# Splitting q and k for the attention scores: three float32r products on row halves in place of one float32 product

## The chip, the cores and the metric

The kernel runs on one core of a Trainium2 chip. The metric is device time in microseconds (us) of one execution; lower is better. TensorE (PE) does the matrix products, VectorE (DVE), ScalarE (ACT) and GpSimd (POOL) the elementwise work, SyncE (SP) issues the DMAs. PEld is the loading of a product's stationary operand.

## The reference

One decoder layer over 16 meta tokens and 1024 tokens, width 1024. A normalized input is projected; half of the result feeds a state-space scan (SSD), the other half stick-breaking attention with 16 heads of 64. Both are normalized and projected out, then comes a gated feed-forward part with a short convolution. The change lies in the attention scores, `zlog` below:

```python
def block(args):                       # one block of 128 queries
    i, qi = args
    zlog = jnp.einsum('bqhd,bkhd->bhqk', qi, kp) * scale
    log_beta = jax.nn.log_sigmoid(zlog)
    log_keep = jnp.where(valid, log_beta - zlog, 0.0)
    after = lax.cumsum(log_keep, axis=3, reverse=True) - log_keep
    w = jnp.where(valid, jnp.exp(log_beta + after), 0.0)
    return jnp.einsum('bhqk,bkhd->bqhd', w, vp)
```

All inputs and the output are float32.

## The kernel before

The large projections are already done in split form: an operand is rounded to float32r (the high part), the rest is a second float32r tile, and three products (high x high, rest x high, high x rest) are summed in PSUM in place of one float32 product (`project_steps`, line 163). The attention scores are plain float32 products.

Heads are worked in eight pairs `p`: head 2p lies on partitions 0 to 63, head 2p+1 on 64 to 127 (`halves`). `qkv_steps` projects q, k and v of a pair in three column chunks each; ACT copies each chunk out of its PSUM bank (`psum_mm`, two banks in turn) to `q` and `k` in SBUF (line 256). The projections of later pairs are a generator, `fill`, which the loops advance by half a chunk at a time so that TensorE has work between the steps of other stages. Pair 0 and part of pair 1 are projected during the last scan stage.

The attention stage loops over `p` and over eight blocks `i` of 128 queries. `block_weights(p, i)` computes the scores of both heads against all keys up to the block, in chunks of up to 456 keys: `z` (PSUM, two buffers of two banks, shared with the transposes `tw`) gets one product for each row half (line 612). ACT takes two sigmoids of it (`kp`, line 613; `bt`, line 614), VectorE runs a reversed scan over `kp` (line 617), GpSimd multiplies (`bt`, line 619). Two blocks later `block_turn` transposes the weights on TensorE (`tw`, line 633) and ACT copies them (`th`); `block_mix` multiplies them with v (`av`, line 647). In this stage the order of TensorE's instructions is the order in which they are written; the other engines' order is chosen by the scheduler when the program is built. Each engine runs its list in order.

The attention pool `ap` takes over the SBUF of the scan stage's pool. `hold` (lines 584 to 586), which the scan over `kp` reads, is the first of its tiles that VectorE writes. The scan stage ends with the store `yd<-zk` of its last chunk (line 544).

Of the kernel before, what the change touches and what calls it, by code (L numbers as in the profile page):

```python
# [8 lines left out]
F32 = mybir.dt.float32  # L9
F32R = mybir.dt.float32r  # L10
BF16 = mybir.dt.bfloat16
AF = mybir.ActivationFunctionType
ALU = mybir.AluOpType
# [3 lines left out]
P = 128  # L17
# [3 lines left out]
NM = 16  # L21
L = NM + T
# [4 lines left out]
NT = T // P  # L27
# [16 lines left out]
def key_chunks(n):  # L44
    m = (n + 511) // 512
    w = -(-n // m)
    w += w % 2
    return [(a, min(w, n - a)) for a in range(0, n, w)]
# [3 lines left out]
def tile_layer(ctx: ExitStack, tc: tile.TileContext, x, meta, rows, parts,  # L52
               w_z, w_xbc, w_dt, w_q, w_k, w_v, w_out, w_up, w_down, out):
    nc = tc.nc
    mm = nc.tensor.matmul
# [22 lines left out]
    def psum_zz(name):  # L78
        return stage[0][1].tile([P, 2, 512], F32, tag="zz", name=name, bufs=2)
# [4 lines left out]
    def psum_tp(name):  # L84
        return stage[0][1].tile([P, 4, P], F32, tag="tp", name=name, bufs=tp_bufs[0])
# [100 lines left out]
    def rstd_of(pool, ss, n, rows_, name):  # L186
        ms = pool.tile([P, n], F32, tag="ms", name=f"ms_{name}", bufs=2)
        nc.vector.tensor_scalar(ms[:rows_], ss, 1.0 / D, EPS, op0=ALU.mult, op1=ALU.add)
        r = pool.tile([P, n], F32, tag="rstd", name=f"rs_{name}", bufs=2)
        nc.gpsimd.tensor_tensor(r[:rows_], ms[:rows_], nhalf[:rows_, :n], op=ALU.pow)  # L190
        return r
# [3 lines left out]
    rp = roll.enter_context(tc.tile_pool(name="roll", bufs=2, side="right"))  # L195
# [5 lines left out]
    with tc.tile_pool(name="pre", bufs=3, side="right") as pre:  # L201
        gpre = row_bcast(pre, 0, D, "gpre")
        for i in range(NT + 1):
            nr = NM if i == 0 else P
            c0 = 0 if i == 0 else NM + (i - 1) * P
# [5 lines left out]
            r = rstd_of(pre, ss[:nr], 1, nr, f"pre{i}")  # L211
# [3 lines left out]
            for hf in range(2):  # L215
# [3 lines left out]
                for b in range(4):  # L219
                    k = 4 * hf + b  # L220
                    nc.tensor.transpose(tp[:, b, :nr], xn[:nr, k * P:(k + 1) * P], ident[:nr, :nr])
                dst = (slice(None), slice(4 * hf, 4 * hf + 4), slice(c0, c0 + nr))
# [4 lines left out]
    halves = (slice(0, 64), slice(64, 128))  # L227
    M0 = NM - 2
    meta_q = rp.tile([P, 8, 32], F32, tag="mtq", name="meta_q", bufs=1)
    meta_k = rp.tile([P, 8, NM], F32, tag="mtk", name="meta_k", bufs=1)  # L230
    nc.gpsimd.memset(meta_q, 0.0)
    heads, state = {}, {}
# [11 lines left out]
    def qkv_block(name, evac, halves_):  # L244
        w = weights_of(name)
        for i, _ in enumerate(project_steps(w, P, xh, xl, CH, evac, name, halves_)):
            if halves_ and i == 1:
                weights_of(name, 1)
            yield

    def qkv_steps(p, post):
        q = rp.tile([P, L + 3], F32, tag="rq", name=f"q{p}", bufs=3)
        k = rp.tile([P, L], F32, tag="rk", name=f"k{p}", bufs=3)
        for dst, nm in ((q, "q"), (k, "k")):
            def ev(acc, c0, n, dst=dst):
                nc.scalar.activation(dst[:, c0:c0 + n], acc[:, :n], AF.Copy)

            yield from qkv_block(f"{nm}{p}", ev, p > 1 or (p, nm) == (1, "k"))
        vt = rp.tile([P, L], F32, tag="rt", name=f"vt{p}", bufs=1)

        def evv(acc, c0, n):
            nc.scalar.activation(vt[:, c0:c0 + n], acc[:, :n], AF.Copy)

        v = rp.tile([P, NT + 1, P], F32, tag="rv", name=f"v{p}")
        vc = rp.tile([P, P], F32, tag="vc", name=f"vc{p}")
        heads[p] = q, k, v, vc
        yield from qkv_block(f"v{p}", evv, p > 0)

        def turn_v(part):
            tp = psum_tp(f"vtp{p}_{part}")  # L270
            for b in range(4):
                c0 = (4 * part + b) * P
                nc.tensor.transpose(tp[:, b, :], vt[:, c0:c0 + P], ident)
            nc.scalar.activation(v[:, 4 * part:4 * part + 4, :], tp, AF.Copy)

        def turn_edge():
            edge = rp.tile([P, NT, NM], F32, tag="edge", name=f"edge{p}", bufs=1)
            nc.vector.tensor_copy(edge[:, :NT - 1, :], vt[:, P:NT * P].rearrange("p (t c) -> p t c", c=P)[:, :, :NM])
            nc.vector.tensor_copy(edge[:, NT - 1, :], vt[:, T:L])
            tp = psum_tp(f"vtc{p}")  # L280
            nc.tensor.transpose(tp[:, 0, :], edge.rearrange("p t c -> p (t c)"), ident)
            nc.scalar.activation(vc, tp[:, 0, :], AF.Copy)
            for j in range(2):
                nc.vector.tensor_copy(meta_q[halves[j], p, 4 * p + 2 * j:4 * p + 2 * j + 2], q[halves[j], M0:NM])
            nc.vector.tensor_copy(meta_k[:, p, :], k[:, 0:NM])
            nc.sync.dma_start(out=mvd[:, p, :], in_=v[:NM, 0, :])

        post += [lambda: turn_v(0), lambda: turn_v(1), turn_edge]

    def qkv_flow(p):  # L290
        post = []
        return qkv_steps(p, post), post
# [13 lines left out]
    with tc.tile_pool(name="ssd", bufs=1, side="right") as sp:  # L306
# [96 lines left out]
        for i in range(NT + 1):  # L403
            nr = NM if i == 0 else P
            c0 = 0 if i == 0 else NM + (i - 1) * P
# [15 lines left out]
        q, adt = e, s2  # L421
# [160 lines left out]
    ap = apool.enter_context(tc.tile_pool(name="attn", bufs=1, side="right"))  # L582
# [9 lines left out]
                                pattern=[[-NM * mul, NT], [col, 32]], channel_multiplier=mul)  # L592
    edges, ys_of = {}, {}

    def block_weights(p, i):
        q, k = heads[p][:2]
        nm = f"{p}_{i}"
        if i == 0:
            edges[p] = ap.tile([P, 2, NT, NM], F32, tag="cb", name=f"cb{p}", bufs=2)
            nc.gpsimd.memset(edges[p][:, :, :, NM - 1:], 0.0)  # L600
        t0, n = NM + i * P, NM + (i + 1) * P
        kpt = ap.tile([P, 2, L], F32, tag="kp", name=f"kp{nm}", bufs=2)
        btt = ap.tile([P, 2, L], F32, tag="bt", name=f"bt{nm}", bufs=3)
        kp, bt = kpt[:, :, 0:n], btt[:, :, 0:n]
        chunks = key_chunks(n)
        for ci, (a, w) in enumerate(chunks):
            if ci == 2:
                yield
            z = psum_zz(f"z{nm}_{ci}")
            for j in range(2):  # L610
                h = halves[j]
                mm(z[:, j, :w], q[h, t0:t0 + P], k[h, a:a + w], start=True, stop=True)  # L612
            nc.scalar.activation(kp[:, :, a:a + w], z[:, :, :w], AF.Sigmoid, scale=-QSCALE)  # L613
            nc.scalar.activation(bt[:, :, a:a + w], z[:, :, :w], AF.Sigmoid, scale=QSCALE)  # L614
        m = n - NM
        for j in range(2):
            nc.vector.tensor_tensor_scan(kp[:, j][:, ::-1], kp[:, j][:, ::-1], hold[:, L - n:L][:, ::-1], 0.0,  # L617
                                         op0=ALU.mult, op1=ALU.max)
            nc.gpsimd.tensor_tensor(bt[:, j, 0:m], bt[:, j, 0:m], kp[:, j, 1:m + 1], op=ALU.mult)  # L619
        nc.gpsimd.tensor_tensor(edges[p][:, :, i, 0:NM - 1], bt[:, :, m:n - 1], kp[:, :, m + 1:n], op=ALU.mult)  # L620
        turn.append((p, i, bt))
# [188 lines left out]
    for p in range(8):  # L810
        for i in range(NT):
            if p == 0 and i == 0:
                run(fill, 1)
            block = block_weights(p, i)
            next(block, None)
            if p > 0 and i == 3:
# [56 lines left out]
    op = opool.enter_context(tc.tile_pool(name="outp", bufs=2, side="right"))  # L873
# [538 lines left out]
    for i in range(2, NFF):  # L1412
        q = probs[i]
        n = probs[i + 1] if i + 1 < NFF else None
# [119 lines left out]
    for s in range(n2):  # L1534
        n, a, b, p = steps2[s]
# [28 lines left out]
        for _ in range(2 if s > 5 and s % 2 else 1):  # L1564
            if wload and (wload[0][0] is not None or s > 5):
                pool, nm, k = wload.pop(0)
# [9 lines left out]
        if p == NPR - 1:  # L1576
            for t in (3, 0, 1, 2):
                todo.append(lambda n=n, t=t, acc=banks[t]: evac2(n, t, acc))
            if n == 6:
                for t in range(4):  # L1580
                    todo.append(lambda t=t: nc.vector.tensor_tensor(facc[0, 1, t], facc[0, 1, t], facc[1, 0, t],
                                                                    op=ALU.add))
# [74 lines left out]
```

## Time and profile before

| | |
|---|---|
| median of 3 runs | 1810.84 us (1809.62 to 1811.23) |
| the profiled execution | 1810.72 us |
| its span, first to last instruction | 1809.0 us |
| mean granted TensorE clock | 0.988 |
| busy: PE / PEld | 1734.8 us (96%) / 1490.1 us (82%) |
| busy: DVE / ACT / POOL | 1061.0 (59%) / 831.3 (46%) / 863.3 us (48%) |
| score products `z`, line 612 | 87.0 us busy, 448 records |

The profile is of one execution. A float32 product appears as two records. The busy time of PE counts overlapping records once, and a record runs from the start to the modelled end of a pipelined product, so what a product costs is read from the starts of its successors. A wait is put down to what came last.

### The profile page before, as it was taken

The numbers are of one execution on the slowest core, as the hardware profiler recorded it, in microseconds if no ns is written. First come the engines' busy times: TensorE is split into PE (matmuls) and PEld (weight loads), VectorE is DVE, ScalarE is ACT, GpSimd is POOL, SyncE is SP. The second block draws the span as 40 slices with busy tenths as digits, with TensorE's granted clock in tenths as the row PEclk, the third lists the DMA queues.
The fourth block names the chain that finished last, engine by engine and source line by source line (L and its number), as shares of the span: only waits on it lengthen the run. The fifth ranks groups of instructions, "written<-read, shape, count | busy, mean of one in ns | idle before, by whom it ended". The sixth has DMA issues, their size and how long they took to land. (4 is left out here: it accounts for less than half of the span.)

```text
span 1809.0 us, 27308 instructions
## 1 busy us (share of the span) xinstructions
PE 1734.8 (96%) x10942; PEld 1490.1 (82%) x10942; DVE 1061.0 (59%) x1125; ACT 831.3 (46%) x1373; POOL 863.3 (48%) x613
## 2 busy tenths in 40 slices
PE   6999999999999999999889899899999999999997
PEld 5899889888888888887567578888899998888886
DVE  5651864873553454455731246766666666657988
ACT  5423563544565565565652334543333333344444
POOL 3213753585555565554752223277777776600001
PEclk9999999999999999999999899999999999999999
DMA  4124333231011011011212545222333332196344
GB/s 157 47 71 131 99 114 118 65 94 42 24 37 36 26 46 36 24 48 61 70 54 76 200 140 174 73 97 88 105 111 105 93 112 88 60 327 220 97 122 158
DMA packets 90547, 173.96 MB, mean 96 GB/s; under 512 B 10698, under 2 KB 35818, under 8 KB 90420
## 3 DMA queue, kind: packets, MB, share of 16 engines
q1 hardware_dynamic: 90420, 172.21, 29.7%
q8 instruction: 86, 1.41, 0.3%
q14 instruction: 41, 0.34, 0.1%
HBM read 122.39 MB, written 49.79 MB: 95 GB/s over the span
## 5 line engine op out<-in xcount | busy, mean ns | idle before, releaser
L617 DVE TENSOR_TENSOR_SCAN kp<-kp,hold 128x272 f32<-128x272 f32 (+7 forms) x128 | 206.8, 1657 | 194.7 <-ACT kp L613 104.5
L619 POOL TENSOR_TENSOR bt<-bt,kp 128x256 f32<-128x256 f32 (+7 forms) x128 | 215.0, 1697 | 189.2 <-DVE kp L617 132.9
L1022 POOL TENSOR_TENSOR wl<-wr,wh 128x1024 fp32r<-128x1024 f32 x44 | 110.7, 2524 | 40.7 <-ACT wh L1021 40.7
L1470 PE MATMUL dn<-dl,dh 128*128 128x512 f32 x308 | 119.9, 389 | 0.1
L1470 PE MATMUL dn<-dh 128*128 128x512 f32 x308 | 119.9, 389 | 0.0
L1470 PE MATMUL dn<-dh,dl 128*128 128x512 f32 x308 | 119.8, 389 | 0.0
L1516 POOL TENSOR_TENSOR fms<-fms,nhalf 128x1 f32<-128x1 f32 x8 | 8.5, 1060 | 225.7 <-DMA ar<-fda 186.0
L613 ACT ACTIVATE kp<-z 128x288 f32<-128x288 f32 (+6 forms) x112 | 82.8, 739 | 56.8 <-PE z L612 33.1
L1399 ACT ACTIVATE dh<-ar 128x512 fp32r<-128x512 f32 x77 | 48.7, 632 | 111.5 <-PE dn L1470 88.9
L612 PE MATMUL z<-k,q 64*128 64x144 f32 (+6 forms) x448 | 87.0, 488 | 13.3 <-ACT bt L614 6.0
L1021 ACT ACTIVATE wh<-wr 128x1024 fp32r<-128x1024 f32 x44 | 46.6, 1060 | 114.7 <-PE fX L1079 68.3
L1151 DVE SCALAR_TENSOR_TENSOR ga<-gr,pp,ga 128x1024 f32<-128x1024 f32 x44 | 71.3, 1622 | 34.8 <-ACT ga L1144 34.0
L635 ACT ACTIVATE th<-tw 128x1024 f32<-128x1024 f32 (+2 forms) x96 | 74.7, 814 | 34.9 <-PE tw L633 33.0
L614 ACT ACTIVATE bt<-z 128x288 f32<-128x288 f32 (+6 forms) x112 | 83.0, 741 | 0.0
L633 PE MATMUL tw<-ident,bt 128*128 128x128 f32 x576 | 78.8, 282 | 3.8 <-issue 2.8
L647 PE MATMUL av<-th,v 128*64 128x128 f32 x1152 | 78.3, 281 | 0.0
L647 PEld LDWEIGHTS av<-th,v 128*64 128x64 f32 x1152 | 62.8, 138 | 18.8 <-issue 17.9
L1400 DVE TENSOR_TENSOR dl<-ar,dh 128x512 fp32r<-128x512 f32 x77 | 53.3, 692 | 42.0 <-ACT dh L1399 42.0
L633 PEld LDWEIGHTS tw<-ident,bt 128*128 128x128 f32 x576 | 63.2, 143 | 15.6 <-issue 13.1
L612 PEld LDWEIGHTS z<-k,q 64*128 64x128 f32 x448 | 36.9, 187 | 41.8 <-issue 18.5
L1470 PEld LDWEIGHTS dn<-dh 128*128 128x128 f32 x308 | 57.8, 188 | 12.3 <-ACT dh L1399 0.3
L1470 PEld LDWEIGHTS dn<-dl,dh 128*128 128x128 f32 x308 | 57.8, 188 | 12.3 <-DVE dl L1400 0.4
(546 smaller groups left out, 5749.2 us busy)
## 6 DMA issues: line engine op xcount, KB each, us to landing
wr<-in_w_up SPq DMA_DIRECT2D x44, 512.0 KB
fds<-ga SPq DMA_DIRECT2D x44, 256.0 KB
b<-in_w_down SPq DMA_DIRECT2D x44, 256.0 KB
ar<-fds SPq DMA_DIRECT2D x44, 256.0 KB
fda<-ga SPq DMA_DIRECT2D x33, 256.0 KB
ar<-fda SPq DMA_DIRECT2D x33, 256.0 KB
yk<-yd SPq DMA_DIRECT2D x16, 512.0 KB
zd<-zt SPq DMA_DIRECT2D x8, 520.0 KB
```

What stands on the lines that cost most here:

```text
L612: mm(z[:, j, :w], q[h, t0:t0 + P], k[h, a:a + w], start=True, stop=True)
L613: nc.scalar.activation(kp[:, :, a:a + w], z[:, :, :w], AF.Sigmoid, scale=-QSCALE)
L614: nc.scalar.activation(bt[:, :, a:a + w], z[:, :, :w], AF.Sigmoid, scale=QSCALE)
L617: nc.vector.tensor_tensor_scan(kp[:, j][:, ::-1], kp[:, j][:, ::-1], hold[:, L - n:L][:, ::-1], 0.0, op0=ALU.mult, op1=ALU.max)
L619: nc.gpsimd.tensor_tensor(bt[:, j, 0:m], bt[:, j, 0:m], kp[:, j, 1:m + 1], op=ALU.mult)
L633: nc.tensor.transpose(tw[:, j, b, :], bt[:, j, c0:c0 + P], ident)
L635: nc.scalar.activation(th[:, :, :nb, :], tw[:, :, :nb, :], AF.Copy)
L647: mm(av[halves[j], :], v[:, kb, halves[j]], th[:, j, b, :], start=kb == 0, stop=kb == i)
L1022: nc.gpsimd.tensor_tensor(l, raw, h.bitcast(F32), op=ALU.subtract)
L1151: nc.vector.scalar_tensor_tensor(v, self.g[jj][:, :, i:i + 256], fconv_w[:, j, i:i + 1], v, op0=ALU.mult, op1=ALU.add)
L1400: sub(lo[:, k], raw, hi[:, k].bitcast(F32), op=ALU.subtract)
L1470: mm(banks[t], u[:, 0, c], v[:, 1, :], start=(p == 0 and i == 0), stop=(p == NPR - 1 and i == 2))
```

## The change

`qkv_steps` rounds k to float32r when ACT copies it out of PSUM (`kh`), and VectorE subtracts that from the same PSUM bank to get the rest (`kl`). `split_q` does the like for the 128 columns of q that a block needs: VectorE copies them rounded (`qh`) and subtracts (`ql`), both in two buffers from the pool `ap`. `block_weights` asks for the next block's pieces after its own score products and before its scan; the first block makes its own. Each score chunk is now three float32r products for each row half, alternating between the halves. `meta_k` is added up again from the two parts.

```diff
     def qkv_steps(p, post):
         q = rp.tile([P, L + 3], F32, tag="rq", name=f"q{p}", bufs=3)
-        k = rp.tile([P, L], F32, tag="rk", name=f"k{p}", bufs=3)
-        for dst, nm in ((q, "q"), (k, "k")):
+        kh = rp.tile([P, L], F32R, tag="rk", name=f"kh{p}", bufs=3)
+        kl = rp.tile([P, L], F32R, tag="rkl", name=f"kl{p}", bufs=3)
+        for dst, nm in ((q, "q"), (kh, "k")):
             def ev(acc, c0, n, dst=dst):
                 nc.scalar.activation(dst[:, c0:c0 + n], acc[:, :n], AF.Copy)
+                if dst is kh:
+                    nc.vector.tensor_tensor(kl[:, c0:c0 + n], acc[:, :n], kh[:, c0:c0 + n].bitcast(F32), op=ALU.subtract)
...
+    def split_q(p, i):
+        q = heads[p][0][:, NM + i * P:NM + (i + 1) * P]
+        qh = ap.tile([P, P], F32R, tag="qh", name=f"qh{p}_{i}", bufs=2)
+        ql = ap.tile([P, P], F32R, tag="ql", name=f"ql{p}_{i}", bufs=2)
+        nc.vector.tensor_copy(qh, q)
+        nc.vector.tensor_tensor(ql, q, qh.bitcast(F32), op=ALU.subtract)
+        qsplit[p, i] = qh, ql
+
     def block_weights(p, i):
-        q, k = heads[p][:2]
+        kh, kl = heads[p][1]
+        if (p, i) not in qsplit:
+            split_q(p, i)
+        qh, ql = qsplit.pop((p, i))
...
             z = psum_zz(f"z{nm}_{ci}")
-            for j in range(2):
-                h = halves[j]
-                mm(z[:, j, :w], q[h, t0:t0 + P], k[h, a:a + w], start=True, stop=True)
+            for s_, (u, r) in enumerate(((qh, kh), (ql, kh), (qh, kl))):
+                for h, j in zip(halves, range(2)):
+                    mm(z[:, j, :w], u[h, :], r[h, a:a + w], start=s_ == 0, stop=s_ == 2)
             nc.scalar.activation(kp[:, :, a:a + w], z[:, :, :w], AF.Sigmoid, scale=-QSCALE)
             nc.scalar.activation(bt[:, :, a:a + w], z[:, :, :w], AF.Sigmoid, scale=QSCALE)
+        nxt = (p, i + 1) if i < NT - 1 else (p + 1, 0)
+        if nxt[0] in heads:
+            split_q(*nxt)
```

More of the change, by code (lines that the diff above doesn't have):

```diff
@@ L265, in qkv_steps @@
         vc = rp.tile([P, P], F32, tag="vc", name=f"vc{p}")
-        heads[p] = q, k, v, vc
+        heads[p] = q, (kh, kl), v, vc
         yield from qkv_block(f"v{p}", evv, p > 0)
@@ L284, in turn_edge @@
                 nc.vector.tensor_copy(meta_q[halves[j], p, 4 * p + 2 * j:4 * p + 2 * j + 2], q[halves[j], M0:NM])
-            nc.vector.tensor_copy(meta_k[:, p, :], k[:, 0:NM])
+            nc.vector.tensor_tensor(meta_k[:, p, :], kh[:, 0:NM].bitcast(F32), kl[:, 0:NM].bitcast(F32), op=ALU.add)
             nc.sync.dma_start(out=mvd[:, p, :], in_=v[:NM, 0, :])
@@ L593, in tile_layer @@
     edges, ys_of = {}, {}
+    qsplit = {}
+    def split_q(p, i):
[5 more added lines that the diff above has]
+        qsplit[p, i] = qh, ql
     def block_weights(p, i):
-        q, k = heads[p][:2]
+        kh, kl = heads[p][1]
         nm = f"{p}_{i}"
+        if (p, i) not in qsplit:
+            split_q(p, i)
+        qh, ql = qsplit.pop((p, i))
         if i == 0:
@@ L600, in block_weights @@
             nc.gpsimd.memset(edges[p][:, :, :, NM - 1:], 0.0)
-        t0, n = NM + i * P, NM + (i + 1) * P
+        n = NM + (i + 1) * P
         kpt = ap.tile([P, 2, L], F32, tag="kp", name=f"kp{nm}", bufs=2)
```

## The prediction

> **What bounds the kernel now.** I read the page first (slices, granted clock), then the busy time by stretches of the attention stage, then what TensorE waits for there.
>
> ```profile
> PE   6999999999999999999889899899999999999997
> PEclk9999999999999999999999899999999999999999
> ```
>
> TensorE works in nearly every slice. The stretches that follow give the window, its length and then the busy us of PE, PEld, DVE, ACT and POOL with counts, the granted clock, and the DMA share.
>
> ```profile
> 480.00:540.00 60.00, 59.71 (x448) 49.86 (x447) 26.56 (x22) 35.81 (x59) 27.04 (x23) 1.00 0.12 37
> 780.00:840.00 60.00, 60.00 (x467) 51.10 (x466) 26.45 (x17) 31.57 (x54) 30.68 (x25) 1.00 0.13 45
> 848.00:864.00 16.00, 11.83 (x98) 6.17 (x94) 15.23 (x8) 14.93 (x24) 14.31 (x9) 1.00 0.11 34
> PE z L612 <- DVE thc L659: 1.5, 5, 0.3
> ```
>
> The last line is from the waits of PE between 480 and 812 us: 1.5 us in 332 is the only wait for another engine on that list. Up to about 840 us the stage is TensorE's; the others are busy near half of the time. Late in head pair 6 this turns: from 848 to 864 ACT and DVE are full and PE has 11.8 us of work in 16.
>
> **What a score chunk costs.** A "chunk" is one `z` tile: both row halves against up to 456 keys. These are rows of the timeline (start, duration, engine, line):
>
> ```profile
> 481.45 0.32 PE L163 MATMUL pj_k<-xh,wh_k 128*128 128x348 f32 x1
> 481.61 0.32 PE L163 MATMUL pj_k<-xl,wh_k 128*128 128x348 f32 x1
> 481.77 0.32 PE L163 MATMUL pj_k<-xh,wl_k 128*128 128x348 f32 x1
> 482.02 0.30 PEld L612 LDWEIGHTS z<-k,q 64*128 64x128 f32 x4 [0.22 <-issue]
> 482.03 0.73 PE L612 MATMUL z<-k,q 64*128 64x272 f32 x4
> 482.69 0.42 PE L163 MATMUL pj_k<-xh,wh_k 128*128 128x348 f32 x1
> ...
> 659.76 1.80 PE L612 MATMUL z<-k,q 64*128 64x456 f32 x8
> 661.49 0.43 PE L163 MATMUL pj_q<-xh,wh_q 128*128 128x346 f32 x1
> ...
> 1135.88 0.28 PE L1093 MATMUL g0a<-b11h,wl 128*128 128x258 f32 x1
> 1135.99 0.28 PE L1093 MATMUL g0a<-b11h,wh 128*128 128x258 f32 x1
> 1136.11 0.29 PE L1093 MATMUL g0a<-b11l,wh 128*128 128x258 f32 x1
> ```
>
> Read starts, not durations, which overlap. One 272-wide chunk holds PE from 482.03 to 482.69, 0.66 us; a pair of 456-wide ones from 659.76 to 661.49, 1.73 us. Each full-precision product is two records; suppose each streams its columns twice and the two halves run side by side, so a chunk passes its width 4 times. The difference, 1.07 us, over 8 x 456 - 4 x 272 = 2560 columns is 0.418 ns a column. That leaves 0.66 - 4 x 272 x 0.418 = 0.21 us fixed, and 1.73 - 8 x 456 x 0.418 = 0.21 for the pair too. So 0.21 us is paid once per run of products (first weight load, draining), and later loads are hidden. Had the halves run one after the other, a column would take half of the 0.418 ns. A rounded (float32r) product streams once: 348 columns start every 0.16 us and 258 every 0.12 us, or 0.418 ns a column plus 0.014 and 0.012 us. I take 0.014 us extra for each.
>
> **What goes and comes on TensorE.** Per chunk of width w, 4 passes become 3 with 0.014 us each: saved 0.418w - 42 ns. A head pair has 14 chunks (144; 272; 400; twice 264, 328, 392 and 456; 348, 348, 344), 4736 columns: 1.98 - 14 x 0.042 = 1.39 us, and 11.1 us over eight pairs. Pairs 0 to 5 are bound by PE: 8.3 us reach the end. In pair 6 only the first three blocks count (0.2); its later ones fall where ACT and DVE are full. Of pair 7 I take 1.0 of 1.4. **Expected gain: 9.5 us,** 0.86 of the 11.1. Bounds for the unseen operation, a float32r product on a row half: without the extra (that of a full-precision pass, nil in the fixed part above) the gain is 0.042 x 14 x 8 x 0.86 = 4.0 larger; if the two halves' extras add up, 4.0 smaller. I keep 0.014, the value of every float32r row.
>
> The fixed 0.21 us, the same after one chunk as after two, says that only a run's first weight load is exposed; with it the result is 1808.3. The Trainium skill, "TensorE: Matmul & The Clock Gate", section "The mechanism" of Part 3 on row and column tiling, says that a load is pulled ahead of running products when its row group differs or when it goes to a background weight buffer, and the list under it names the row group as the only case. Here a half's next load always meets its own row group; by that list the result would be the 1834 of the exposed-load rival below.
>
> **What comes on VectorE.** 64 blocks get a rounding copy and a subtraction, 24 chunks of k a subtraction out of PSUM.
>
> ```profile
> L107 DVE CAST lowr<-low 128x128 fp32r<-128x128 f32 x1 | 0.2, 227 | 0.2 <-POOL low L104 0.2
> L486 DVE TENSOR_TENSOR cbm<-cb,tri 128x128 f32<-128x128 f32 x16 | 4.5, 284 | 3.2 <-PE cb L484 3.1
> L224 DVE TENSOR_TENSOR xl<-xtp,xh 128x512 fp32r<-128x512 f32 x16 | 9.9, 679 | 0.6 <-ACT xh L223 0.6
> L224 DVE TENSOR_TENSOR xl<-xtp,xh 128x64 fp32r<-128x64 f32 x2 | 0.3, 216 | 0.0
> ```
>
> Mean ns stands behind the bar's first number. The copy is 0.227 us and the subtraction at most 0.284: 64 x 0.511 = 33 us. The PSUM subtraction of 346 columns lies between 0.216 (64) and 0.679 (512), by the line through them 0.51: 24 x 0.51 = 12 us. These 45 us spread over a stage of more than 400 us (the rows quoted run from 420 to 864) in which VectorE is busy under half of the time until 840, so I cost them at nothing as work; that cover is gone only behind 848, where a late scan would delay a block's turn that is read two blocks on. Two places remain to be looked at. First, k's PSUM bank is now freed by VectorE, in order behind its scans, not by ACT alone. The tightest place I found:
>
> ```profile
> 673.52 9.98 DVE L617 TENSOR_TENSOR_SCAN kp<-kp,hold 128x1040 f32<-128x1040 f32 x4 [5.87 <-issue]
> ...
> 679.40 0.47 ACT L256 ACTIVATE k<-pj_k 128x348 f32<-128x348 f32 x1 [1.32 <-PE pj_k L163]
> ...
> 686.91 0.42 PE L163 MATMUL pj_k<-xh,wh_k 128*128 128x346 f32 x1
> ```
>
> ACT is done at 679.87, the scans at 683.50, so the subtraction ends near 684.0; the bank (two in turn) is wanted by the chunk that begins at 686.91. 2.9 us remain: nothing is lost. Second, each block's q pieces are made a block ahead, before the scan of the block before, and are not waited for, except in the very first block.
>
> **The first block.** There is nothing ahead of it. In the built program VectorE's list is: the fill of `hold`, the copy `qh0_0`, the second write of `hold`, then `ql0_0`. In before, the same place looks so:
>
> ```profile
> 418.06 0.69 DVE L542 TENSOR_TENSOR zk<-yt,zk 128x512 f32<-128x512 f32 x1 [4.17 <-PE yt L540]
> ...
> 419.79 1.21 SPq L544 DMA_DIRECT2D yd<-zk  x1
> ...
> 419.98 0.52 PE L612 MATMUL z<-k,q 64*128 64x144 f32 x4
> ...
> 420.42 0.43 PE L163 MATMUL pj_k<-xh,wh_k 128*128 128x348 f32 x1
> ...
> 423.91 0.49 DVE L585 MEMSET hold<- 128x520 uint32 x1 [5.15 <-DMA yd<-zk]
> 424.43 0.49 DVE L586 CAST hold<-ident 128x128 bf16<-128x128 f32 x1
> ```
>
> `hold` lies in memory that the scan stage's last store, `yd<-zk`, is still reading; VectorE waits 5.15 us for its landing, and nobody minded: the first scores need only q and k and run at 419.98, and PE goes on with projections. After the change the first scores need `qh0_0` and `ql0_0`, which stand behind that fill. Hold at 423.91 to 424.40, copy to about 424.6, second `hold` write, `ql` to about 425.3; then a 144-wide product's three passes and the drain, so the projection that began at 420.42 begins at about 425.8. PE's order is written out by hand, and the rest of pair 1's projections is queued behind these scores: **5.4 us lost**, in a stretch where PE waited for nothing.
>
> The gap also costs clock. Rows of before: two gaps and the granted clock (the number behind POOL's) in and after them.
>
> ```profile
> 872.32 1.52 PE L612 MATMUL z<-k,q 64*128 64x344 f32 x4 [4.72 <-ACT bt L614]
> 871.90:878.60 6.70, 6.28 (x37) 5.01 (x37) 6.70 (x4) 5.04 (x11) 6.70 (x4) 0.50 0.00 0
> ...
> 1141.91 0.58 PE L1093 MATMUL g0a<-b21h,wh 128*128 128x258 f32 x1 [4.52 <-ACT gr L1099]
> 1141.60:1144.90 3.30, 2.98 (x14) 2.99 (x15) 2.59 (x3) 1.79 (x4) 0.54 (x1) 0.50 0.08 34
> ```
>
> After idle times of 4.7 and 4.5 us PE ran at half clock until 878.6 and 1144.9, 6.3 and 3.0 us past its restart, which costs half of that, 3.1 and 1.5 us. After dense projections I take 1.6 us (bounds 0.5 and 3.1).
>
> **Sum:** -9.5 + 5.4 + 1.6 = -2.5 us. The profiled execution took 1810.7 us (span 1809.0), the median is 1810.84, so one stands for the other: 1808.3 us. By the bounds: -13.5 + 5.9 = -7.6 at best, -5.5 + 8.5 = +3.0 at worst. A measurement of this kernel can tell about 0.2% (3.6 us) from no change; the forecast lies within it.
>
> **Rivals.**
> - *No gap at the first block* (the store lands sooner, or the pieces get ahead of `hold`). Against it: the order of VectorE's list and the 5.15 us. Then -9.5: 1801.3. Chance 0.10.
> - *Slower: the row halves' float32r products run one after the other.* For it: no float32r product on 64 rows is in the trace; against it: the full-precision halves ran side by side. Each chunk then streams 6 widths and six extras instead of 4 widths: 0.836w + 84 ns, 3.96 + 1.18 = 5.1 us a pair, 41 in all, 35 at the 0.86 that counts, with the gap 42: 1853. It decides as soon as the second half starts more than one width behind the first. Chance 0.07.
> - *Exposed loads:* the second pair of loads in the 0.30 us row starts 0.11 us behind the first. At 0.11 for each of the 34 passes of a pair that are not first in their run, 3.7 us against 1.39 saved: +2.3 a pair, 16 counted, with the gap +23: 1834. Chance 0.05.
> - *VectorE's queue:* if it ran 4 us later than before, the bank above would be late, and if 8 us, the 21 chunks of k in the stage (pair 0's three lie ahead of it) by about 1 us each: 21 + 7.0 - 9.5, 1829. Chance 0.04.
> - *The gain does not reach the end* (ACT's sigmoids take over as PE quickens): +7.0, 1817.8. Against it: ACT's 36 us in 60. Chance 0.04.
>
> **How the numbers follow.** The forecast has 0.70: of it 0.22 below -3.6 us, 0.46 within, 0.02 above. Faster 0.22 + 0.10 = 0.32; same 0.46; slower 0.02 + 0.20 = 0.22. The range 1801 to 1818 takes in the forecast's bounds, the first rival and the last (0.84).
>
> **What would show it.** In the profile after: a lone 272-wide chunk holds PE 0.59 us instead of 0.66 and the 456-wide pair 1.44 instead of 1.73; one PE idle time of about 5 us near 420 us, ended by DVE `qh` or `ql`, with clock 0.50 behind it; no PE wait for `kl`. Wrong would be chunks above 0.7 us, waits of projections for VectorE, or no gap.

## The result and the profile after

| | before | after |
|---|---|---|
| median | 1811.23 us (5 runs, 1809.62 to 1812.90) | 1818.34 us (5 runs, 1816.88 to 1819.24) |
| ratio to before, 95% interval | | 1.0038 [1.0027, 1.0049] |
| the profiled execution, its span | 1810.72, 1809.0 us | 1819.03, 1817.3 us |
| mean granted TensorE clock | 0.988 | 0.980 |

The changed kernel is 7.1 us slower; 1808.3 was forecast, with 1818 as the upper end of the range. First the score chunks. These are rows of TensorE's timeline after (start, duration, engine, line, operation): the first block, a lone 272-wide chunk, and a pair of 456-wide ones.

```profile
424.93 0.49 PE L628 MATMUL z<-kh,qh 64*128 64x144 f32 x2 [5.25 <-DVE qh L604]
425.36 0.49 PE L628 MATMUL z<-kh,ql 64*128 64x144 f32 x2
425.65 0.41 PE L628 MATMUL z<-kl,qh 64*128 64x144 f32 x2
425.99 0.66 PE L163 MATMUL pj_k<-xh,wh_k 128*128 128x348 f32 x1
...
489.81 0.40 PE L628 MATMUL z<-kh,qh 64*128 64x272 f32 x2
490.04 0.28 PE L628 MATMUL z<-kh,ql 64*128 64x272 f32 x2
490.17 0.28 PE L628 MATMUL z<-kl,qh 64*128 64x272 f32 x2
490.38 0.42 PE L163 MATMUL pj_k<-xh,wh_k 128*128 128x348 f32 x1
...
664.12 0.48 PE L628 MATMUL z<-kh,qh 64*128 64x456 f32 x2
...
665.25 0.37 PE L628 MATMUL z<-kl,qh 64*128 64x456 f32 x2
665.55 0.43 PE L163 MATMUL pj_q<-xh,wh_q 128*128 128x346 f32 x1
```

The 272-wide chunk holds TensorE from 489.81 to 490.38, 0.57 us (before 0.66); the pair from 664.12 to 665.55, 1.43 us (before 1.73). Each row holds both halves' products (x2). The second and third pass of the 272-wide chunk start 0.13 us apart, which is one half's 272 columns at 0.418 ns and the extra, so the halves run side by side. The gap stands at the first block: 5.25 us, released by `qh`. VectorE's rows there:

```profile
424.11 0.49 DVE L588 MEMSET hold<- 128x520 uint32 x1 [5.72 <-DMA yd<-zk]
424.52 0.20 DVE L604 CAST qh<-q 128x128 fp32r<-128x128 f32 x1
424.63 0.49 DVE L589 CAST hold<-ident 128x128 bf16<-128x128 f32 x1
425.03 0.28 DVE L605 TENSOR_TENSOR ql<-q,qh 128x128 fp32r<-128x128 f32 x1
```

The order is the one that the prediction read out of the built program. From there to 845 us these are TensorE's only waits (in total, times, longest):

```profile
PE z L628 <- DVE qh L604: 5.3, 1, 5.3
PE z L628 <- DVE thc L678: 2.3, 6, 0.4
```

No wait for `kl`. Late in head pair 6 it is different. Busy time by windows (length, then PE, PEld, DVE, ACT, POOL, granted clock, DMA share, GB/s), 840 to 900 us, before and then after:

```profile
840.00:900.00 60.00, 48.62 (x344) 32.61 (x342) 45.77 (x28) 44.41 (x72) 44.04 (x26) 0.94 0.24 76
```
```profile
840.00:900.00 60.00, 45.13 (x361) 33.22 (x357) 51.13 (x42) 44.16 (x71) 41.16 (x26) 0.89 0.23 75
```

VectorE is busy 5.4 us more in these 60 us, TensorE 3.5 us less, and the granted clock falls from 0.94 to 0.89. The path there, in rows of the timelines, before and then after:

```profile
866.96 4.04 DVE L617 TENSOR_TENSOR_SCAN kp<-kp,hold 128x912 f32<-128x912 f32 x2
869.22 6.05 POOL L619 TENSOR_TENSOR bt<-bt,kp 128x896 f32<-128x896 f32 x2 [2.08 <-DVE kp L617]
876.42 3.35 POOL L773 TENSOR_TENSOR yl<-yk,yh 128x1024 fp32r<-128x1024 f32 x1
879.83 0.50 PE L783 MATMUL mo<-woha,yl 128*128 128x512 f32 x1 [0.72 <-POOL yl L773]
```
```profile
869.69 4.00 DVE L636 TENSOR_TENSOR_SCAN kp<-kp,hold 128x912 f32<-128x912 f32 x2
871.91 6.06 POOL L638 TENSOR_TENSOR bt<-bt,kp 128x896 f32<-128x896 f32 x2 [2.55 <-DVE kp L636]
879.11 3.33 POOL L792 TENSOR_TENSOR yl<-yk,yh 128x1024 fp32r<-128x1024 f32 x1
880.17 2.35 DVE L604 CAST qh<-q 128x128 fp32r<-128x128 f32 x1
882.49 0.80 PE L802 MATMUL mo<-woha,yl 128*128 128x512 f32 x1 [3.90 <-POOL yl L792]
```

The scan of block (6,6) starts 2.7 us later, GpSimd's multiplication waits for it, GpSimd's `yl` (the rest of the output projection's operand) stands behind that, and TensorE's `mo` product waits for `yl`: 2.7 us later too. Not all of the 2.7 us arises here: the scores of block (6,5) already start 1.1 us later in this execution (1.4 by the count of the table below), so VectorE's queue adds some 1.6. After this longer wait, and at other places, TensorE runs at half clock. Four such windows of after that before does not have:

```profile
423.70:430.50 6.80, 5.57 (x21) 5.33 (x22) 3.51 (x13) 2.46 (x4) 2.76 (x10) 0.50 0.01 4
444.20:447.60 3.40, 3.40 (x18) 3.16 (x15) 2.00 (x4) 2.12 (x4) 1.99 (x3) 0.50 0.52 154
881.10:887.90 6.80, 5.41 (x13) 4.30 (x14) 6.16 (x4) 1.78 (x2) 3.99 (x2) 0.50 0.24 78
925.50:932.30 6.80, 6.28 (x35) 4.78 (x32) 5.32 (x6) 3.99 (x6) 4.72 (x4) 0.50 0.01 2
```

### The profile page after: what moved, and what is told of

It is laid out like the page before. It is cut to its first block, busy times and chain, and to the rows that moved or that the text cites. A ratio compares the mean times of both kernels' runs of the same rounds, so it can differ in the third digit from the quotient of the medians.

```text
span 1817.3 us, 27933 instructions
## 1 busy us (share of the span) xinstructions
PE 1733.9 (95%) x11166; PEld 1514.3 (83%) x11166; DVE 1117.8 (62%) x1277; ACT 831.0 (46%) x1373; POOL 858.1 (47%) x613
## 3 DMA queue, kind: packets, MB, share of 16 engines
q8 instruction: 88, 1.44, 0.3%
## 5 line engine op out<-in xcount | busy, mean ns | idle before, releaser
L636 DVE TENSOR_TENSOR_SCAN kp<-kp,hold 128x272 f32<-128x272 f32 (+7 forms) x128 | 184.5, 1483 | 31.4 <-ACT kp L629 24.2
L604 DVE CAST qh<-q 128x128 fp32r<-128x128 f32 x64 | 36.5, 570 | 99.6 <-PE z L628 99.4
L1489 PEld LDWEIGHTS dn<-dh,dl 128*128 128x128 f32 x308 | 57.8, 188 | 12.1
```

Source lines behind the costliest of these rows:

```text
L1489: mm(banks[t], u[:, 0, c], v[:, 1, :], start=(p == 0 and i == 0), stop=(p == NPR - 1 and i == 2))
```

## The experiments

The table follows each profiled execution along the stage. It shows how much later than in before the first score product of a block starts, counted from the last transpose ahead of the stage (`vtc`), since the executions arrive there between 417.7 and 421.2 us. "Half clock" is the total length of stretches at 0.50 between 840 and 1160 us; before has 23.9 us. One execution each; the medians stand with the experiments.

| kernel | (0,0) | (0,5) | (6,5) | (7,0) | (7,5) | end | half clock |
|---|---|---|---|---|---|---|---|
| after | +5.3 | +9.0 | +1.4 | +5.5 | +5.3 | +8.7 | 41.0 |
| first block's pieces ahead | 0.0 | +1.7 | -5.9 | -1.6 | -1.8 | +1.6 | 37.5 |
| late pieces ahead, gap kept | +5.3 | +9.0 | +1.4 | +3.1 | +4.2 | +8.2 | 47.8 |
| both ahead | 0.0 | +1.6 | -6.0 | -4.2 | -4.5 | -4.7 | 27.3 |
| products only | 0.0 | -0.4 | -8.0 | -8.0 | -8.2 | -3.7 | 34.1 |
| k's rests only | 0.0 | +1.7 | -5.8 | -5.7 | -5.9 | -1.7 | 41.0 |
| VectorE only | 0.0 | +6.3 | +6.3 | +6.3 | +7.7 | +8.5 | 27.3 |
| gap only | +5.3 | +9.5 | +9.5 | +9.5 | +9.5 | +9.8 | 20.5 |
| both ahead, kept busy | 0.0 | +1.5 | -6.1 | -5.8 | -7.6 | -7.8 | 20.5 |
| gap, late ahead, kept busy | +5.4 | +9.0 | +1.4 | +1.6 | -0.2 | +2.2 | 20.5 |
| products only, kept busy | 0.0 | -0.5 | -8.0 | -6.6 | -8.4 | -4.9 | 30.7 |
| before, kept busy | 0.0 | +0.1 | +0.1 | +2.6 | +1.0 | +2.5 | 23.9 |

**1. The first block's pieces ahead of `hold`**, in the pool `rp` instead of `ap`, so that they wait for no store.

```diff
+    split_q(0, 0)
     tp_bufs[0] = 1
     psum_stage("psB")
...
-        qh = ap.tile([P, P], F32R, tag="qh", name=f"qh{p}_{i}", bufs=2)
-        ql = ap.tile([P, P], F32R, tag="ql", name=f"ql{p}_{i}", bufs=2)
+        qh = rp.tile([P, P], F32R, tag="qh", name=f"qh{p}_{i}", bufs=2)
+        ql = rp.tile([P, P], F32R, tag="ql", name=f"ql{p}_{i}", bufs=2)
```

> The changed kernel with q's pieces in the long-lived pool instead of the attention pool, and those of the very first block made before the fill of hold. Theory (the trace after): the wait before the first scores cost 5.6 us and the half clock behind it 2.0, in all 7.6 us from the first block on, plus perhaps 1.3 us of a second half-clock window at 444 us; all of it goes: 1809 to 1811 us against 1818.3, with no PE idle time near 420 us. Rival (the late stretch of pair 6 is set by VectorE, ScalarE and DMAs and absorbs what comes earlier): 1815 to 1818.

1811.25 us, ratio to before 0.9998 [0.9990, 1.0007], just above the expected 1809 to 1811 and far from the rival's 1815. The gap and its clock are 7.1 us of the median (1818.34 less 1811.25). Of the 1.7 us at (0,5) only 0.3 are a wait (for `kl`); for the rest see the last section.

**2. The gap alone**: before, with the first block's q copied behind `hold`.

```diff
+        if (p, i) == (0, 0):
+            q0 = ap.tile([P, P], F32, tag="q0", name="q0")
+            nc.vector.tensor_copy(q0, q[:, t0:t0 + P])
...
+                u = q0[h, :] if (p, i) == (0, 0) else q[h, t0:t0 + P]
-                mm(z[:, j, :w], q[h, t0:t0 + P], k[h, a:a + w], start=True, stop=True)
+                mm(z[:, j, :w], u, k[h, a:a + w], start=True, stop=True)
```

> The kernel before, full-precision scores, with one thing added: the first block's q columns are copied by VectorE into a tile of the attention pool, behind the fill of hold, and the first scores read the copy. My theory (the gap alone, 4.9 us of waiting and about 2.5 us of half clock, is carried unchanged to the end): 1811.3 + 7.1 = 1818.4 us, 1817 to 1820. Rival (the later ACT- and VectorE-bound stretch of pair 6 swallows part of it): 1814 to 1816.

1820.67 us beside 1812.14, ratio 1.0045 [1.0031, 1.0058]: 8.5 us, more than the 7.1 expected, and the table carries it unchanged from (0,5) to the end; nothing swallows it. TensorE's wait for it:

```profile
PE z L616 <- DVE q L604: 5.3, 1, 5.3
```

**3. TensorE's part alone**: q and k rounded when ACT copies them, three products of the rounded parts, nothing for VectorE; the rests are left out of the scores.

The lines of the scores against those of after:

```diff
...
-            for s_, (u, r) in enumerate(((qh, kh), (ql, kh), (qh, kl))):
+            for s_, (u, r) in enumerate(((qh, kh), (qh, kh), (qh, kh))):
...
```

> TensorE's side alone: q and k are rounded when they leave PSUM, no rests are made, and each score chunk is three products of the rounded parts (the two rest products are replaced by repeats of the first, so that the scores are not the reference's). No VectorE work is added and no gap made. Prediction's term: 9.5 us faster than before, 1801.7; if pair 7 gives nothing 1803; if the products on row halves had cost what the full-precision ones do, 1811.

1806.56 us, ratio 0.9970 [0.9959, 0.9981]: 4.8 us gained, half of the forecast. The table says where the other half went: 8.0 us are there at (6,5), 8.2 at (7,5), and only 3.7 at the end, with 10.2 us more of half clock than before. The clock is not a matter of that one execution: its seven runs were granted 0.980 to 0.985 on average over the span, the 21 runs of before 0.985 to 0.989.

**4. k's rests on top**: as 3, with `kl` by VectorE; q's rest is left out of the scores.

```diff
...
-            for s_, (u, r) in enumerate(((qh, kh), (ql, kh), (qh, kl))):
+            for s_, (u, r) in enumerate(((qh, kh), (qh, kh), (qh, kl))):
...
```

> The changed kernel without q's rests and pieces: q is rounded once when it is copied out of PSUM and the products are q x kh, q x kh, q x kl (q's rest is left out of the scores). VectorE's subtraction for kl stays. My theory (the subtraction out of PSUM is hidden, only the q pieces cost): as with no VectorE work at all, 1806.6 us, 1804.5 to 1808.5, and no PE wait for kl. Rival (the bank that VectorE frees late holds PE, as the 2.5 us wait for kl in the VectorE-only kernel might mean): 1809 to 1811 with PE waits for kl.

1808.51 us beside 1812.14, ratio 0.9979 [0.9970, 0.9988], at the upper edge of the expected 1804.5 to 1808.5; its interval overlaps that of experiment 3. TensorE waited for `kl` once, 0.4 us. By (0,5) it stands 2.1 us behind experiment 3, most of it in a window of half clock that the last section takes up. Only 0.1 us is lost between (6,5) and (7,0), where after loses 4.1: k's rests have no part in that.

**5. VectorE's part alone**: rests and pieces made as in after, scores in full precision that don't read them (`kh` is then k unrounded, so the rests are zeros that take the same work).

```diff
...
-            for s_, (u, r) in enumerate(((qh, kh), (ql, kh), (qh, kl))):
-                for h, j in zip(halves, range(2)):
-                    mm(z[:, j, :w], u[h, :], r[h, a:a + w], start=s_ == 0, stop=s_ == 2)
+            for j in range(2):
+                h = halves[j]
+                mm(z[:, j, :w], heads[p][0][h, t0:t0 + P], kh[h, a:a + w], start=True, stop=True)
...
```

> VectorE's side alone: the rests of k and both pieces of q are made as in the changed kernel, but the scores stay full-precision products of q and k that do not read them. Theory: no gap at the first block; VectorE is 2 to 3 us late in pair 6, PE waits for yl and loses 3 to 5 us: 1814 to 1816. Rival (that work is hidden, as predicted): 1811 within 1 us.

1816.95 us, ratio 1.0037 [1.0025, 1.0049]. The number lies 1 us above the expected 1814 to 1816, but for another reason, so it doesn't count for the theory. Pieces that nobody reads were all made early, in one heap, and `kl` of pair 1 came behind them:

```profile
437.33 0.49 DVE L259 TENSOR_TENSOR kl<-pj_k,kh 128x346 fp32r<-128x346 f32 x1
...
437.88 3.69 PE L301 MATMUL pta<-ones,sq 128*2 128x1 f32 x18 [2.46 <-DVE kl L259]
```

So the loss lies at the beginning (6.3 us by (0,5)), and pair 6 had no pieces left. What it does show is that a late `kl` holds TensorE through the bank.

**6. The late pieces ahead as well**: as 1, with the pieces of blocks (6,4) to (6,7) and (7,0) made at (6,2), where VectorE has time, in two slots of q and k that are free by then.

```diff
...
+        if (p, i) == (6, 2):
+            split_ahead()
...
```

> As e1_first_ahead, and q's pieces of pair 6's blocks 4 to 7 and of pair 7's block 0 made in one go at pair 6's block 2, ahead of the stretch in which VectorE is full. Theory (VectorE ran 2.7 us late there, GpSimd's yl came 2.7 us later, PE waited 3.9 us for it and ran at half clock behind: 5.2 us): another 3 to 5 us below e1_first_ahead, 1804 to 1807. Rival (the wait for yl comes from somewhere else, the row loads of yd for example): the same as e1_first_ahead within 1 us.

1806.54 us, ratio 0.9977 [0.9965, 0.9990]: 4.7 us less than experiment 1 (the two intervals only touch). Between (6,5) and (7,0) 1.8 us are lost instead of 4.3, and TensorE's wait for `yl` is 2.2 us instead of 3.7 (in experiment 3 there is none).

**7. The late pieces ahead, the gap kept**: the edit of 6 on the changed kernel itself.

```diff
...
+        if (p, i) == (6, 2):
+            split_ahead()
...
```

> The changed kernel with its gap at the first block, but the q pieces of pair 6 blocks 4 to 7 and of block (7,0) made at block (6,2). My theory (two separate losses that add: the gap 7.1 us, VectorE's late queue in pair 6 4.7 us): 1818.3 - 4.7 = 1813.6 us, 1812 to 1815, and z(7,0) no later against before than z(6,7) is. Rival (the late queue costs only because the kernel is out of step with its transfers after the gap): as the changed kernel without its gap gave it, no help here, 1818.

1817.81 us beside 1812.14, ratio 1.0032 [1.0019, 1.0044], not the 1812 to 1815 expected but the rival's 1818. The place behaved as forecast (1.7 us lost between (6,5) and (7,0), after 4.1), but behind (7,0) this execution lost 5.1 us more, with 47.8 us of half clock. The losses do not simply add. Whether the rival's reason holds (out of step with the transfers) or the clock, experiment 10 asks.

**8. TensorE kept busy**: as 6, with 35 products into a bank that nobody reads, placed ahead of four waits.

```diff
+    def keep_busy(n):
+        spare = psum_tp("spare").rearrange("p a b -> p (a b)")
+        kh = heads[7][1][0]
+        for _ in range(n):
+            mm(spare, kh[:, 0:P], kh[:, 0:512], start=True, stop=True)
...
+            if (p, i, ci) == (7, 3, 1):
+                keep_busy(8)
...
+            if (p, i) == (6, 7):
+                keep_busy(13)
             run(block)
...
+            if (p, i) == (6, 6):
+                keep_busy(7)
...
+            if (p, i) == (6, 7):
+                keep_busy(7)
             run(first, int(p == 7 and (i % 2 or i > 5) or p == 6 and i == 7))
```

> The version with both groups of pieces made ahead (1806.54 us), with 35 further products of 512 columns into a PSUM bank that nobody reads, put ahead of four waits of PE of 2.1 to 3.8 us in pairs 6 and 7. My theory (what is missing from the forecast gain of 9.5 us is half clock after these waits): the half-clock windows between 855 and 903 us go, and although PE has 8 us more to do the time falls to 1802 to 1804.5. Rival (the gain ends at the work of ACT, VectorE and GpSimd there, the clock does not matter): 1806.5, or 1 to 3 us more where the added products lie on the path.

1804.49 us beside 1812.14, ratio 0.9955 [0.9942, 0.9967]: 7.7 us below before, with more work than experiment 6, whose interval it overlaps by a hair (0.9965 to 0.9967). The same 25 us of pair 6, first of 6 and then of this kernel:

```profile
860.00:885.00 25.00, 18.54 (x140) 15.10 (x140) 20.10 (x10) 16.20 (x29) 21.01 (x9) 0.86 0.15 43
```
```profile
860.00:885.00 25.00, 22.05 (x166) 17.90 (x166) 21.09 (x11) 17.20 (x30) 20.80 (x9) 0.93 0.10 27
```

**9. The filling on before and on the products-only kernel**, 17 products at (6,7) and 8 at (7,3); in before they are 128 columns wide, in full precision.

```diff
...
+            if (p, i, ci) == (7, 3, 1):
+                keep_busy(8)
...
+            if (p, i) == (6, 7):
+                keep_busy(17)
             run(block)
...
```

> The kernel before, full-precision scores, with only the added products: 17 before PE's wait for ACT in block (6,7) (4.7 us) and 8 before its wait in (7,3) (2.3 us), each of 128 columns in full precision, about 0.22 us, into a bank that nobody reads. My theory (half clock follows these two waits in every such kernel, and the profile of before shows 6.8 and 3.4 us of it behind them): 2 to 3.5 us less than before; then some 3 of the 7.7 us that the version with both groups ahead and the added products gained belong to the added products, not to the split. Rival (the filling only pays because a quicker TensorE waits more): no change, within 1 us of before.

1812.23 us beside 1810.67, ratio 1.0007 [0.9998, 1.0016]: no gain, the rival's case. In before the filling only moved the wait: `mo` then waited 2.5 us for `yl`, and half clock came there.

> The products-only version (q and k rounded, three products of the rounded parts, no rests; so the rests are left out of the scores) with 17 and 8 products of 512 columns added ahead of its waits of 4.9 us in (6,7) and 2.4 us in (7,3). My theory (its gain stood at 8.5 us at block (7,5) and was lost to half clock): 7.5 to 9.5 us less than before instead of 4.8. Rival (ACT, VectorE and GpSimd set the pace there): 4 to 6 us less than before, as without them.

1803.99 us beside 1810.67, ratio 0.9965 [0.9953, 0.9978]: 6.7 us by the medians, and the interval reaches into both expectations, so undecided. In its profile 8.4 us stand at (7,5) and 5.9 at (7,6), with a 6.8 us window at half clock between them, behind small waits that had not been filled.

**10. The gap with everything else mended**: as 8, with the first block's pieces behind `hold` again.

```diff
-        qh = rp.tile([P, P], F32R, tag="qh", name=f"qh{p}_{i}", bufs=2)
-        ql = rp.tile([P, P], F32R, tag="ql", name=f"ql{p}_{i}", bufs=2)
+        qh = ap.tile([P, P], F32R, tag="qh", name=f"qh{p}_{i}", bufs=2)
+        ql = ap.tile([P, P], F32R, tag="ql", name=f"ql{p}_{i}", bufs=2)
...
-    split_q(0, 0)
```

> The best version (both groups of pieces ahead, added products in pairs 6 and 7; 7.7 us less than before) with only the first block's pieces back behind the fill of hold, so with the gap. My theory (the gap costs its 7.1 to 8.5 us whatever stands behind it, and what ate the 4.7 us in the version with the late pieces ahead and the gap was half clock in pairs 6 and 7): 7.1 to 8.5 less 7.7, so within 1.5 us of before, about 1811. Rival (with the gap in place the late pieces' gain does not come, for a reason other than the clock): 4 to 6 us more than before, as that version, 1815 to 1817.

1812.78 us beside 1811.41, ratio 1.0005 [0.9996, 1.0014], 1.4 us above before: as the theory had it. Against experiment 8 the gap costs 9.0 us, and against 7 the filling brings 4.3. So the gap takes 7.1 to 9.0 us whatever is done in pair 6 (experiments 1, 2 and this one), and most of what was missing in 7 comes back when TensorE is kept busy: half clock falls from 47.8 to 20.5 us. The rival's reason in 7 is not needed for that, though no run here changes the transfers.

**11. The price of a piece**, measured behind the last store of before; the core of the second probe:

```diff
+        for w in (1024, 256):
...
+            for _ in range(16 if w > 256 else 40):
+                nc.gpsimd.tensor_tensor(c[:, 0:w], a[:, 0:w], b[:, 0:w], op=ALU.mult)
+            for _ in range(12):
+                nc.vector.tensor_tensor(pl, bank, ph.bitcast(F32), op=ALU.subtract)
+            for _ in range(4):
+                nc.vector.tensor_copy(ph, back[:, 0:P])
+                nc.vector.tensor_tensor(pl, back[:, 0:P], ph.bitcast(F32), op=ALU.subtract)
+            for _ in range(4):
+                nc.vector.tensor_copy(ph, bank)
```

> The kernel before with a measurement behind its last store: 8 pairs of rounding copy and subtraction of 128 columns in SBUF and 8 subtractions that read a PSUM bank, on VectorE, first with GpSimd idle, then the same beside 12 GpSimd multiplications of 1024 columns. My theory (VectorE and GpSimd get in each other's way at SBUF): 0.23 and 0.29 us alone, beside GpSimd 0.8 to 0.9 us in the mean for copy and subtraction in SBUF, and no change (within 10%) for the subtraction out of PSUM. Rival (the copies in pair 6 were long for another reason, such as the transfers of that time): no difference between the two halves. The time of the whole is not compared.

> The kernel before with a second measurement behind its last store: beside GpSimd multiplications of 1024 columns, and then of 256, VectorE does 12 subtractions that read a PSUM bank, 4 pairs of rounding copy and subtraction in SBUF, and 4 rounding copies out of PSUM. My theory (a VectorE instruction with both operands in SBUF, or a copy from SBUF to SBUF, waits until the GpSimd instruction that is under way has ended, so it costs one GpSimd instruction whatever its own size): SBUF copies and subtractions of 128 columns take 2.3 to 2.5 us beside 1024 columns and 0.6 to 0.7 us beside 256; what reads PSUM stays at 0.3 us beside both. Rival (the bandwidth is shared, each slows the other in proportion): the same length, near 2.4 us, beside both sizes, and the reads of PSUM are also slowed. The time of the whole is not compared.

Two of VectorE's rows in the first probe, GpSimd idle:

```profile
1812.64 0.23 DVE L1615 CAST pbh<-back 128x128 fp32r<-128x128 f32 x1
1812.90 0.29 DVE L1616 TENSOR_TENSOR pbl<-back,pbh 128x128 fp32r<-128x128 f32 x1
```

Beside GpSimd the first probe's copies and subtractions took 2.25 to 2.45 us, far more than the 0.8 to 0.9 expected. Its reads of PSUM beside GpSimd came too late: the multiplications had ended. The second probe has them. First the GpSimd rows (16 multiplications of 1024 columns, 2.41 us each; 40 of 256, 0.80 us each), then VectorE's beside them:

```profile
1813.46 38.60 POOL L1618 TENSOR_TENSOR pbc<-pba,pbb 128x1024 f32<-128x1024 f32 x16 [9.73 <-DVE pbl L1620]
1852.87 31.94 POOL L1618 TENSOR_TENSOR pbc<-pba,pbb 128x256 f32<-128x256 f32 x40 [0.81 <-DVE pbb L1616]
...
1813.16 3.86 DVE L1620 TENSOR_TENSOR pbl<-bank,pbh 128x128 fp32r<-128x128 f32 x12
1825.66 2.32 DVE L1622 CAST pbh<-back 128x128 fp32r<-128x128 f32 x1
1828.01 2.45 DVE L1623 TENSOR_TENSOR pbl<-back,pbh 128x128 fp32r<-128x128 f32 x1
1852.70 3.86 DVE L1620 TENSOR_TENSOR pbl<-bank,pbh 128x128 fp32r<-128x128 f32 x12
1857.78 0.70 DVE L1622 CAST pbh<-back 128x128 fp32r<-128x128 f32 x1
1858.52 0.83 DVE L1623 TENSOR_TENSOR pbl<-back,pbh 128x128 fp32r<-128x128 f32 x1
```

In SBUF the same 128 columns take as long as one GpSimd instruction lasts, whatever that is: each of these four rows starts within 0.1 us behind the start of one; the first copy of the second probe, which starts in the middle of one, takes 1.26 us and ends with it. The twelve subtractions out of PSUM take 3.86 us beside both.

## Why the prediction was right and wrong

**Score chunks: right.** 0.57 and 1.43 us for a forecast 0.59 and 1.44. In the products-only kernel the blocks from (0,0) to (6,0) come 7.8 us sooner, 1.30 us a pair (1.39 forecast). The halves run side by side and a run's later loads are hidden; the two slower rivals on TensorE are out. For the list in the Trainium skill ("TensorE: Matmul & The Clock Gate", "The mechanism" of Part 3) the trace of after disagrees as that of before did: loads that meet their own row half cost nothing visible.

**First block: right in place and mechanism, a little low in size.** 5.3 us of waiting for 5.4. The clock behind it cost 2.4 us by (0,3) in after (that block starts 7.75 us late by the table's count, less 5.3), for 1.6 forecast with bounds 0.5 and 3.1. Forecast 7.0 in all; 7.1 (experiment 1), 8.5 (2) and 9.0 (10) measured.

**`kl` and its bank: right.** 0.51 us each as forecast, and no wait in after (one of 0.3 and one of 0.4 us in experiments 1 and 4). The rival on VectorE's queue had a late VectorE too, but at this bank, where nothing was lost.

**VectorE's 45 us "at nothing as work": the step that failed first.** It failed twice. The size: the groups of after are

```profile
L604 DVE CAST qh<-q 128x128 fp32r<-128x128 f32 x64 | 36.5, 570 | 99.6 <-PE z L628 99.4
...
L605 DVE TENSOR_TENSOR ql<-q,qh 128x128 fp32r<-128x128 f32 x64 | 34.4, 538 | 2.0
```

70.9 us for the pieces, where 33 were forecast. The price that the prediction took, from a copy outside the stage, hid it: in after a copy took 0.23 us with GpSimd quiet and up to 2.35 beside it. The 18 of the 64 copies that lasted over 0.45 us all end within 0.1 us of the end of the GpSimd instruction that was under way. The trace of before had the warning, in a row of VectorE's groups that the prediction passed over: a copy of two columns in the same stage that takes 1.4 us in the mean.

```profile
L284 DVE COPY meta_q<-q 64x2 f32<-64x2 f32 x12 | 17.0, 1418 | 0.6 <-ACT q L256 0.5
```

And the place: "that cover is gone only behind 848, where a late scan would delay a block's turn that is read two blocks on" named the right stretch and the wrong reader. The late scan delayed GpSimd's multiplication, GpSimd works in order, and `yl` for TensorE stood behind it. Moving these pieces out of that stretch (experiment 6 against 1) gave back 4.7 us in the median. The two profiles differ by 6.3 us at the end: 2.5 arise between (6,5) and (7,0), some 1.5 of these in the wait for `yl`; 3.6 arise behind (7,0), where half clock is the likely taker (37.5 against 27.3 us in all), which these two runs alone don't show.

**The gain of 9.5 us: mis-sized, the second step that failed.** 8.0 us had been earned by (6,5), for 8.5 forecast (8.3 in pairs 0 to 5 and 0.2). At the end of the products-only kernel 4.8 were left in the median. The prediction charged half clock only to the wait that the change adds, but pair 6 and what follows are full of waits of 0.4 to 5 us in before and in products-only alike, and with less to do between them TensorE fell to half clock more often in products-only: 34.1 us instead of 23.9. That the clock takes gain is shown where filling brought gain (10 against 7, 4.3 us; 8 against 6, 2.9 us, with intervals that just overlap); the filling brought nothing in before, and less than expected on the products alone, so how much of the missing 4.7 us is clock and how much is the pace of the other engines stays open for that kernel.

**The sum.** Taking the parts out one after another, by medians: gap +7.1 (after less experiment 1), VectorE's work +4.7 (1 less 3), products -4.8 (3 less before). The forecast had +7.0, 0 and -9.5. These three make up the 7.1 us by construction; taken out in another order (7) they don't keep their sizes, since each changes where the waits of pairs 6 and 7 fall. The result's 1818.3 is also what the rival "the gain does not reach the end" gave, but not by its mechanism: ACT took nothing over (TensorE's two waits for its `bt` between 838 and 935 us sum to 5.0 us in before, 5.3 in after).

## What to carry to other kernels

Before an engine's added work is called hidden, look at the longest of its short copies in the same stage, not at a mean from elsewhere, and follow a late instruction through every in-order queue up to TensorE. Where one product replaces a slower one, count the gain only up to the first stretch with waits: there a quicker TensorE may get half clock for it. A first consumer that is moved behind a fill of reused memory waits for that memory's last reader; here two small tiles in another pool were worth 7 us.

## What the runs showed of the hardware

**VectorE and GpSimd at SBUF.** A 128-column copy or subtraction in SBUF lasted 2.3 to 2.5 us beside GpSimd instructions of 2.41 us, 0.70 and 0.83 beside 0.80, and 0.23 and 0.29 alone; with PSUM as a source, 0.29 us in every case. It is a wait until the GpSimd instruction under way has ended (1.26 us where the copy began in its middle), not a shared bandwidth. The Trainium skill, "SBUF — State Buffer", section "Who interferes with whom", says just this: whichever of the two starts first holds the shared ports for its whole instruction and the other fully blocks, while a VectorE instruction with at most one SBUF input outside the 2-port modes does not contend. The runs agree in every row of VectorE's. That VectorE also holds up GpSimd the probes do not show: GpSimd's 1024-column multiplications start every 2.42 us with VectorE's pieces beside them and without.

**Half clock without a wait.** In experiment 1 TensorE waited for nothing around 435 us, and yet:

```profile
432.30:435.70 3.40, 3.40 (x35) 3.02 (x34) 0.44 (x3) 0.53 (x2) 3.40 (x4) 1.00 0.02 5
435.70:439.10 3.40, 3.40 (x14) 3.33 (x12) 2.36 (x4) 1.97 (x4) 1.98 (x2) 0.51 0.49 154
```

The first window holds 18 products of one column (`pta`, 2.07 us); the second ran at half clock, some 1.3 us lost. Before has the same products without it. And a stretch need not be idle throughout; in experiment 6, around a wait of 2.4 us:

```profile
896.50:899.90 3.40, 0.98 (x8) 0.54 (x9) 3.27 (x4) 1.41 (x4) 2.41 (x3) 1.00 0.42 152
899.90:903.30 3.40, 3.38 (x19) 2.46 (x20) 1.70 (x4) 1.83 (x3) 0.91 (x2) 0.50 0.08 27
```

All stretches at half clock last a multiple of 3.41 us (but for the last of each trace, which the trace's end cuts off), and in each trace they all start on one grid of 3.41 us, which lies differently from trace to trace. That sorts the case of `pta`: where its 18 products lie within one cell of the grid (after and experiments 1, 2, 4, 6, 7, 8 and 10, eight traces), half clock follows at the end of the cell; where an edge of the grid falls among them (before, experiment 3 and both of 9, four traces), it doesn't. Experiment 5 has a wait there and does not count.

The Trainium skill, "TensorE: Matmul & The Clock Gate", section "What's actually happening", gives the same length and says that the window runs free of the kernel, and that half clock follows an idle window. The length agrees; that a window must be idle does not: 0.98 us of work in 3.4, or one-column products without a pause, were followed by half clock too. A grid that lies anew in each execution would also explain why kernels with many waits spread more (experiment 6: 1804.1 to 1811.7 us); no run here sets where it lies, so that is argued, not shown.
